# State-space constants: four 16-row products per step on four column groups of TensorE, after the step's four transposes

## The chip, the cores and the metric

One core of one Trainium2 chip runs the whole program. The metric is the device time of one execution in microseconds (us), lower is better. The kernel before has three timed runs and one profiled execution.

## The reference

The program is two transformer-like blocks on a sequence of 512 rows and 1024 columns. The change lies in the constants of the second block's state-space mixer (S5): 64 groups, each with 64 complex states and 16 inputs and outputs.

```python
def s5_mixer(u, lam_re, lam_im, log_dt, b_re, b_im, c_re, c_im, d_skip, w_glu):
    ...
    mag = jnp.exp(lr * dt)
    ab_re = mag * jnp.cos(li * dt)
    ab_im = mag * jnp.sin(li * dt)
    ...
    bb_re = coef_re[..., None] * br - coef_im[..., None] * bi
    bb_im = coef_re[..., None] * bi + coef_im[..., None] * br
    v_re = jnp.einsum('blgh,gph->blgp', uf, bb_re)
    v_im = jnp.einsum('blgh,gph->blgp', uf, bb_im)
    ...
    _, _, s_re, s_im = lax.associative_scan(_complex_affine_combine, (a_re, a_im, v_re, v_im), axis=1)
    y = (jnp.einsum('blgp,ghp->blgh', s_re, c_re.astype(jnp.float32))
         - jnp.einsum('blgp,ghp->blgh', s_im, c_im.astype(jnp.float32))
         + d_skip.astype(jnp.float32).reshape(SSM_GROUPS, SSM_GROUP) * uf)
```

The kernel runs the scan in chunks of 8 positions. For every group it needs three constant matrices that depend on the weights alone: the pole's powers times B (what a chunk's inputs add to the state), C times the pole's powers (what the state adds to a chunk's outputs), and the products C·A^l·B for l = 0 to 7, 16×16 each, with the skip weight d on the diagonal of the first (what a chunk's inputs add to its own outputs).

## The kernel before

`run` (L1616) calls `block1` and then `block2`. Work on large matrices follows one pattern: a weight tile is loaded by a DMA that SyncE (SP) issues (L98), split into a high part (ScalarE, ACT, L131) and a low part (VectorE, DVE, L132), and three matmuls (L126 to L128) make one product of nearly full precision. In the first block's feed-forward part, `up_prod` (48 matmuls for both matrices, 24 for one) alternates with bias, convolution and gate on ACT and DVE, and eight down-products of 33 matmuls follow each half.

The state-space constants are prepared in between. `s5_prep` (L987) is a generator. The feed-forward loop calls `next(prep)` at two out of every five up-products (L833, L834) and at three of the eight down-products of the first half (L852, L853), so TensorE gets one small piece of the preparation between long pieces of matmul work. There are 16 steps; a step takes GC = 4 groups:

- `front(c)` (L1007) runs on GpSimd (POOL). It makes `W`, the pole's powers times B (128×4×8×16), and `Ca`, C times the powers (128×4×9×16). Both have two buffers, so POOL works one step ahead of TensorE.
- `back(c)` (L1060) runs one call later. It writes `Ca` to `MO_d` (L1064), and per group lets TensorE do a transpose of `W` (L1071, 128×128, into `ps`) and the product of `W`'s first 16 columns with `Ca` (L1072, 16 rows × 128 columns, into `pk`, f32, no split). The four groups of a step alternate: transpose, product, transpose, product. ACT copies `ps` to `Rc` (L1074) and `pk` to `kp` (L1075); POOL writes `Rc` to `R_d` (L1076), makes the diagonal `dg` from `dT` (L1078), adds it (L1079), and writes `kp` to `K_d` (L1080).

Every second step also starts with two transposes of the next C rows (L1053). At the end eight DMAs (L1101) copy shifted pieces of `K_d` to `MO_d`. `R_d` and `MO_d` are read in `block2`, from `s5_state` and `s5_out`.

The order on each engine is set by a scheduler in the tile framework from the program's order and dependences, and instructions of one engine run in that order.

At the end of the first block the row sums of squares are made (`ss_mix`, L878) and `rstd_rows` (L311) turns them into 1/sqrt on DVE (`rsqrt_dve`, L160 to L166, `nwx`, `nwi`, `nwt`, `rstd`) and spreads them with matmuls (L322) and copies (L326, L327) to `rb_mix`, by which the first products of the second block are scaled (L1177). `block2` also has 25 small DVE instructions on 128×8 and 128×16 tiles for a lower bound (`lbm`, `lbd`, `ex`, `lbc`, `oml`, L892 to L905 and L1153 to L1161), which use no result of this neighbourhood.

Of the kernel before, what the change touches and what calls it, by code (L numbers as in the profile page):

```python
# [11 lines left out]
F32 = mybir.dt.float32  # L12
# [3 lines left out]
ALU = mybir.AluOpType  # L16
AX = mybir.AxisListType
PSUM = bass.MemoryType.PSUM

P = 128  # L20
# [49 lines left out]
class Kern:  # L70
# [837 lines left out]
    def s5_poles(self):  # L908
        nc, tc, A = self.nc, self.tc, self.A
        v = nc.vector  # L910
        self.R_d = tc.dram_tile([P, 64, P], F32, name="R_d")
        self.MO_d = tc.dram_tile([P, 64, 2 * P], F32, name="MO_d")
        NP = 18
        pt = self.s5pt = self.tmp.tile([P, NP, 64], F32, name="s5pt")
        dT = self.s5dT = self.tmp.tile([16, 64], F32, name="s5dT")
        if True:
            if True:
                dp = self.s5dpool
                t = lambda s: dp.tile([64, 64], F32, name="s5_" + s)
                lr, li, th, sn, ve = t("lr"), t("li"), t("th"), t("sn"), t("ve")  # L920
                ld, dt = dp.tile([64, 1], F32, name="s5_ld"), dp.tile([64, 1], F32, name="s5_dt")
                dd = self.s5dd = self.tmp.tile([64, 16], F32, name="s5_dd")
                nc.gpsimd.dma_start(lr, A["ssm_lambda_re_2"][0])
                nc.gpsimd.dma_start(li, A["ssm_lambda_im_2"][0])
                nc.gpsimd.dma_start(ld, A["ssm_log_dt_2"].rearrange("o g -> g o"))
                nc.gpsimd.dma_start(dd, A["ssm_d_2"][0].rearrange("(g h) -> g h", h=16))
                e2, p = self.expm1_parts(dp, ld, 64, 1)
                v.scalar_tensor_tensor(dt, p, 1.0, e2, ALU.add, ALU.mult)
                x, em = t("x"), t("em")
                v.tensor_scalar(x, lr, dt, None, ALU.mult)  # L930
                v.tensor_scalar(th, li, dt, None, ALU.mult)
                e2, p = self.expm1_parts(dp, x, 64, 64)
                v.tensor_tensor(em, p, e2, ALU.mult)
                v.scalar_tensor_tensor(em, e2, -1.0, em, ALU.add, ALU.add)
                self.sincos(dp, th, sn, ve, 64, parts=64)
                cs, nr, den, u1, u2 = t("cs"), t("nr"), t("den"), t("u1"), t("u2")
                q = dp.tile([64, NP, 1, 64], F32, name="s5_q")
                v.tensor_scalar(cs, ve, -1.0, 1.0, ALU.mult, ALU.add)
                v.tensor_tensor(nr, em, cs, ALU.mult)
                v.tensor_tensor(nr, nr, ve, ALU.subtract)  # L940
                ar, ai = q[:, 0, 0], q[:, 1, 0]
                v.tensor_scalar(ar, nr, 1.0, None, ALU.add)
                v.scalar_tensor_tensor(ai, em, 1.0, sn, ALU.add, ALU.mult)
                v.tensor_tensor(den, lr, lr, ALU.mult)
                v.tensor_tensor(u1, li, li, ALU.mult)
                v.tensor_tensor(den, den, u1, ALU.add)
                v.reciprocal(den, den)
                cr, ci = q[:, 16, 0], q[:, 17, 0]
                v.tensor_tensor(u1, nr, lr, ALU.mult)
                v.tensor_tensor(u2, ai, li, ALU.mult)  # L950
                v.tensor_tensor(u1, u1, u2, ALU.add)
                v.tensor_tensor(cr, u1, den, ALU.mult)
                v.tensor_tensor(u1, ai, lr, ALU.mult)
                v.tensor_tensor(u2, nr, li, ALU.mult)
                v.tensor_tensor(u1, u1, u2, ALU.subtract)
                v.tensor_tensor(ci, u1, den, ALU.mult)
                for l in range(2, 9):
                    a, b = l // 2, l - l // 2
                    (xr, xi), (yr, yi) = [(q[:, 2 * m - 2, 0], q[:, 2 * m - 1, 0]) for m in (a, b)]
                    zr, zi = q[:, 2 * l - 2, 0], q[:, 2 * l - 1, 0]  # L960
                    v.tensor_tensor(u1, xr, yr, ALU.mult)
                    v.tensor_tensor(u2, xi, yi, ALU.mult)
                    v.tensor_tensor(zr, u1, u2, ALU.subtract)
                    v.tensor_tensor(u1, xr, yi, ALU.mult)
                    v.tensor_tensor(u2, xi, yr, ALU.mult)
                    v.tensor_tensor(zi, u1, u2, ALU.add)
                self.s5q = q
# [19 lines left out]
    def s5_prep(self):  # L987
        nc, tc, A, pt, dT = self.nc, self.tc, self.A, self.s5pt, self.s5dT
        if True:
            sp = self.s5pool  # L990
            GC = 4
            g = nc.gpsimd
# [6 lines left out]
            g.dma_start(bw[64:], bre)  # L999
            g.tensor_scalar(bw[:64], bw[:64], -1.0, None, ALU.mult)  # L1000
            cre, cim = [A[n][0].rearrange("(c g) h p -> (g h) c p", c=8) for n in ("ssm_c_re_2", "ssm_c_im_2")]
            K_d = tc.dram_tile([16, 64, 240], F32, name="K_d")
            kp = sp.tile([16, GC, 240], F32, name="s5_kp")
            g.memset(kp, 0.0)
            cs8 = None

            def front(c):  # L1007
# [36 lines left out]
            def c_load(c2):  # L1044
                raw = craw[c2] = sp.tile([P, 3, 64], F32, tag="s5_cr", bufs=2, name=self.nm("s5cr"))
                for i, src in enumerate((cre, cim, cre)):
                    nc.sync.dma_start(raw[:, i], src[:, c2])

            def c_rows(c2):
                raw = craw.pop(c2)  # L1050
                ps = self.aux()
                for i in range(2):
                    nc.tensor.transpose(ps[:, i * P : i * P + P], raw[:, i : i + 2].rearrange("p a b -> p (a b)"), self.ident)  # L1053
                cs = nxt[c2] = sp.tile([P, 2, 8, 16], F32, tag="s5_cs8", bufs=2, name=self.nm("s5cs8"))
                p4 = ps[:, : 2 * P].rearrange("p (s g h) -> p s g h", s=2, h=16)
                nc.scalar.copy(cs[:64, 0], p4[:64, 0])
                nc.scalar.mul(cs[64:, 0], p4[64:, 0], -1.0)
                nc.scalar.mul(cs[:, 1], p4[:, 1], -1.0)

            def back(c, W, Ca):  # L1060
                g0 = c * GC
                gs = slice(g0, g0 + GC)
                tl = lambda s, shp, b=1: sp.tile(shp, F32, tag="s5_" + s, bufs=b, name=self.nm("s5" + s))
                g.dma_start(self.MO_d[:, gs, P:].rearrange("p g (l h) -> p g l h", h=16), Ca[:, :, 1:, :])  # L1064
                Rc = tl("Rc", [P, GC, P])
                for h in range(GC // 4):
                    ps = self.aux()
                    pk = self.aux()
                    for i in range(4):
                        gi = 4 * h + i  # L1070
                        nc.tensor.transpose(ps[:, i * P : i * P + P], W[:, gi].rearrange("p l h -> p (l h)"), self.ident)  # L1071
                        nc.tensor.matmul(pk[:16, i * P : i * P + P], lhsT=W[:, gi, 0, :], rhs=Ca[:, gi, :8, :].rearrange("p l h -> p (l h)"), start=True, stop=True)  # L1072
                    hs = slice(4 * h, 4 * h + 4)
                    nc.scalar.copy(Rc[:, hs], ps.rearrange("p (g x) -> p g x", g=4))  # L1074
                    nc.scalar.copy(kp[:, hs, 112:], pk[:16].rearrange("p (g x) -> p g x", g=4))  # L1075
                g.dma_start(self.R_d[:, gs], Rc)  # L1076
                dg = tl("dg", [16, GC, 16])
                g.tensor_tensor(dg, self.ident[:16, :16].unsqueeze(1).to_broadcast([16, GC, 16]), dT[:, gs].unsqueeze(2).to_broadcast([16, GC, 16]), ALU.mult)  # L1078
                g.tensor_tensor(kp[:, :, 112:128], kp[:, :, 112:128], dg, ALU.add)  # L1079
                g.dma_start(K_d[:, gs], kp)  # L1080

            prev = None
            c_load(0)
# [2 lines left out]
            for c in range(17):  # L1086
                yield
                if c == 0:
                    ps = self.aux()
                    nc.tensor.transpose(ps[:16, :64], self.s5dd, self.ident[:64, :64])  # L1090
                    nc.vector.tensor_copy(dT, ps[:16, :64])
                if c % 2 == 0 and c < 14:
                    c_load(c // 2 + 1)
                if c % 2 and c < 15:
                    c_rows(c // 2 + 1)
                if prev is not None:
                    back(c - 1, *prev)
                prev = front(c) if c < 16 else None
            yield
            for j in range(8):  # L1100
                g.dma_start(self.MO_d[16 * j : 16 * j + 16, :, :P], K_d[:, :, 16 * j : 16 * j + P])  # L1101


    def slot(self):
# [571 lines left out]
```

## Time and profile before

| what | value |
|---|---|
| median of three runs | 1825.73 us (1822.69, 1825.73, 1832.12) |
| profiled execution, its own time | 1825.45 us |
| its span, first to last instruction | 1823.6 us |
| TensorE matmul (PE) busy | 1738.0 us, 95% |
| VectorE / ScalarE / GpSimd busy | 59% / 43% / 18% |
| mean granted TensorE clock | 0.986 of full speed |

The profiled execution is 2 us longer than its span, and lies within 0.3 us of the median. PE is a matmul and PEld a weight load on TensorE; the two overlap, and a matmul's duration holds its latency, so what a stream of matmuls costs is read from start to start. "issue" as a releaser means that the engine waited for nothing that the profile shows.

### The profile page before, as it was taken

The numbers are of one execution on the slowest core, as the hardware profiler recorded it, in microseconds if no ns is written. First come the engines' busy times: TensorE is split into PE (matmuls) and PEld (weight loads), VectorE is DVE, ScalarE is ACT, GpSimd is POOL, SyncE is SP. The second block draws the span as 40 slices with busy tenths as digits, with TensorE's granted clock in tenths as the row PEclk, the third lists the DMA queues.
The fourth block names the chain that finished last, engine by engine and source line by source line (L and its number), as shares of the span: only waits on it lengthen the run. The fifth ranks groups of instructions, "written<-read, shape, count | busy, mean of one in ns | idle before, by whom it ended". The sixth has DMA issues, their size and how long they took to land.

```text
span 1823.6 us, 28508 instructions
## 1 busy us (share of the span) xinstructions
PE 1738.0 (95%) x11509; PEld 1525.5 (84%) x11509; DVE 1074.7 (59%) x2343; ACT 780.4 (43%) x1298; POOL 321.4 (18%) x441
## 2 busy tenths in 40 slices
PE   1989998999999999999999999999999999999998
PEld 1777755877777778899899899899999999889986
DVE  6687878986443566454488634343444466536652
ACT  2674485344332444324546834343322443324332
POOL 5000000278836841031000000200000000000001
PEclk9899998999999999999899999999999999999999
DMA  7323625353244325367432135936443222332231
GB/s 280 98 88 111 215 71 186 116 105 124 85 117 150 108 92 182 117 195 123 129 99 82 65 116 162 227 118 232 156 137 104 82 93 70 113 107 93 70 104 47
DMA packets 178766, 226.64 MB, mean 124 GB/s; under 512 B 10699, under 2 KB 146746, under 8 KB 175178
## 3 DMA queue, kind: packets, MB, share of 16 engines
q1 hardware_dynamic: 164256, 181.95, 31.5%
q0 software_dynamic: 10640, 38.19, 7.8%
q10 hardware_dynamic: 3738, 4.69, 0.7%
q8 instruction: 90, 1.47, 0.4%
q14 instruction: 42, 0.34, 0.1%
HBM read 196.29 MB, written 32.70 MB: 126 GB/s over the span
## 4 chain that ended last, share of the span: by engine, by line
PE 69%; issue 12%; DVE 9%; ACT 4%; DMA 4%; POOL 1%; ACTq 0%; SPq 0%; POOLq 0%; DVEq 0%
PE pp L126 18%; PE pp L127 17%; PE pp L128 17%; DVE wl L132 2%; DMA wraw<-in_w_in_dram 2%; PE pd L128 1%; PE pd L126 1%; PE pd L127 1%; PE aux L1072 1%; PE aux L1354 1%; PE aux L442 1%; PE aux L126 1%; PE aux L128 1%; PE aux L127 1%; PE pv L455 1%
## 5 line engine op out<-in xcount | busy, mean ns | idle before, releaser
L126 PE MATMUL pp<-s,wh 128*128 128x258 f32 (+2 forms) x1856 | 543.2, 293 | 8.6 <-ACT sg L1427 4.5
L127 PE MATMUL pp<-s,wh 128*128 128x258 f32 (+2 forms) x1856 | 527.9, 284 | 0.0
L128 PE MATMUL pp<-s,wl 128*128 128x258 f32 (+2 forms) x1856 | 525.5, 283 | 0.0
L132 DVE TENSOR_TENSOR wl<-wraw,wh 128x1024 fp32r<-128x1024 f32 (+4 forms) x260 | 302.9, 1178 | 190.4 <-ACT wh L131 189.4
L131 ACT CAST wh<-wraw 128x1024 fp32r<-128x1024 f32 (+4 forms) x260 | 245.0, 964 | 338.0 <-PE pp L127 203.4
L126 PEld LDWEIGHTS pp<-s,wh 128*128 128x128 f32 x1856 | 352.2, 190 | 13.3 <-ACT sg L1427 4.7
L127 PEld LDWEIGHTS pp<-s,wh 128*128 128x128 f32 x1856 | 352.9, 190 | 0.2 <-DVE s L333 0.2
L128 PEld LDWEIGHTS pp<-s,wl 128*128 128x128 f32 x1856 | 352.4, 190 | 0.1
L126 PE MATMUL pp<-h2H,wh 128*128 128x512 f32 x336 | 133.5, 397 | 2.4 <-DVE cy L846 2.4
L127 PE MATMUL pp<-h2L,wh 128*128 128x512 f32 x336 | 133.2, 396 | 1.1 <-DVE h2L L343 1.1
L128 PE MATMUL pp<-h2H,wl 128*128 128x512 f32 x336 | 132.1, 393 | 0.0
L126 PEld LDWEIGHTS pp<-h2H,wh 128*128 128x128 f32 x336 | 63.1, 188 | 20.1 <-ACT aH L131 2.8
L127 PEld LDWEIGHTS pp<-h2L,wh 128*128 128x128 f32 x336 | 63.0, 188 | 16.1 <-DVE h2L L343 2.2
L128 PEld LDWEIGHTS pp<-h2H,wl 128*128 128x128 f32 x336 | 63.2, 188 | 14.2
L126 PE MATMUL pp<-aH,wh 128*128 128x512 f32 x176 | 70.1, 398 | 0.0
L127 PE MATMUL pp<-aL,wh 128*128 128x512 f32 x176 | 69.8, 396 | 0.0
L128 PE MATMUL pp<-aH,wl 128*128 128x512 f32 x176 | 69.8, 396 | 0.0
L1592 POOL TENSOR_TENSOR ht<-ht,gf 128x512 f32<-128x512 f32 x4 | 5.7, 1438 | 344.7 <-ACT fsq L1590 344.7
L126 PE MATMUL pp<-wh,hH 128*128 128x512 f32 (+1 forms) x160 | 62.3, 389 | 1.2 <-ACT hH L525 1.2
L1556 DVE TENSOR_TENSOR xz<-pp,rb_f 128x516 f32<-128x516 f32 x44 | 30.6, 696 | 54.2 <-PE pp L128 54.2
L127 PE MATMUL pp<-wl,hH 128*128 128x512 f32 (+1 forms) x160 | 61.9, 387 | 0.5 <-DVE wl L132 0.5
L128 PE MATMUL pp<-wh,hL 128*128 128x512 f32 (+1 forms) x160 | 61.4, 384 | 0.0
(592 smaller groups left out, 3462.0 us busy)
## 6 DMA issues: line engine op xcount, KB each, us to landing
wraw<-in_w_up_dram SPq DMA_DIRECT2D x40, 1024.0 KB, 5.2
wada<-in_w_ada_dram SPq DMA_DIRECT2D x24, 1024.0 KB, 4.9
wraw<-in_w_in_dram SPq DMA_DIRECT2D x17, 1024.0 KB, 12.3
wraw<-in_w_down_dram SPq DMA_DIRECT2D x16, 704.0 KB, 4.6
wraw<-in_w_in_dram SPq DMA_DIRECT2D x22, 512.0 KB, 5.4
wraw<-in_w_down_dram SPq DMA_DIRECT2D x8, 1024.0 KB
wraw<-MO_d SPq DMA_DIRECT2D x6, 896.0 KB
xraw<-in_w_in_dram SPq DMA_DIRECT2D x10, 512.0 KB, 7.7
```

The costliest lines, as they stand in the source:

```text
L126: mm(ps, lhsT=sh, rhs=mh, start=start, stop=False)
L127: mm(ps, lhsT=sh, rhs=ml, start=False, stop=False)
L128: mm(ps, lhsT=sl, rhs=mh, start=False, stop=stop)
L131: self.nc.scalar.copy(H, x)
L132: self.nc.vector.tensor_tensor(L, x, H.bitcast(F32), ALU.subtract)
L442: nc.tensor.transpose(ps[:, w : w + P], probs[i][:, j * P : (j + 1) * P], self.ident)
L455: self.nc.tensor.matmul(pv[64 * a : 64 * a + 64, j * P :], lhsT=vs[a](j), rhs=ptrs[a][j], start=(j == 0), stop=(j == NT - 1), skip_group_c ...
L1072: nc.tensor.matmul(pk[:16, i * P : i * P + P], lhsT=W[:, gi, 0, :], rhs=Ca[:, gi, :8, :].rearrange("p l h -> p (l h)"), start=True, stop=True)
L1354: nc.tensor.matmul(p3[:n, c, 32 * i : 32 * i + 32], lhsT=lhs, rhs=ch(Q1)[:, c, 32 * i : 32 * i + 32], start=True, stop=True)
L1556: nc.vector.tensor_tensor(xz, ps, rb, ALU.mult)
L1592: nc.gpsimd.tensor_tensor(h, h, gf[:, :512], ALU.mult)
```

## The change

A step's four transposes now come first, and its four products after them. Each product takes 32 columns of `W` (two powers, of which the second is not used) and writes to its own 32 partitions of one PSUM tile, so that each uses its own quarter of TensorE's columns. `kp`, `dg`, `dT` and `K_d` are laid out accordingly: group i of a step on partitions 32i to 32i+15, the other 16 rows unused. The copy of the products is 128×128 and no longer 16×512; the write to `K_d` has 128 rows of 240 and no longer 16 rows of 960. A constant `eye` (four 32×32 unit matrices, one above the other) is made once by a DVE reduction.

```diff
-        dT = self.s5dT = self.tmp.tile([16, 64], F32, name="s5dT")
+        dT = self.s5dT = self.tmp.tile([P, 16], F32, name="s5dT")
...
-                dd = self.s5dd = self.tmp.tile([64, 16], F32, name="s5_dd")
+                dd = self.s5dd = self.tmp.tile([16, 4, 32], F32, name="s5_dd")
+                nc.gpsimd.memset(dd, 0.0)
...
-            K_d = tc.dram_tile([16, 64, 240], F32, name="K_d")
-            kp = sp.tile([16, GC, 240], F32, name="s5_kp")
+            K_d = tc.dram_tile([16, P, 240], F32, name="K_d")
+            kp = sp.tile([P, 240], F32, name="s5_kp")
             g.memset(kp, 0.0)
+            eye = sp.tile([P, 32], F32, name="s5_eye")
+            nc.vector.tensor_reduce(eye, self.ident.rearrange("p (i r) -> p r i", r=32), AX.X, ALU.add)
...
-                for h in range(GC // 4):
-                    ps = self.aux()
-                    pk = self.aux()
-                    for i in range(4):
-                        gi = 4 * h + i
-                        nc.tensor.transpose(ps[:, i * P : i * P + P], W[:, gi].rearrange("p l h -> p (l h)"), self.ident)
-                        nc.tensor.matmul(pk[:16, i * P : i * P + P], lhsT=W[:, gi, 0, :], rhs=Ca[:, gi, :8, :].rearrange("p l h -> p (l h)"), start=True, stop=True)
-                    hs = slice(4 * h, 4 * h + 4)
-                    nc.scalar.copy(Rc[:, hs], ps.rearrange("p (g x) -> p g x", g=4))
-                    nc.scalar.copy(kp[:, hs, 112:], pk[:16].rearrange("p (g x) -> p g x", g=4))
+                ps = self.aux()
+                pk = self.aux()
+                for i in range(GC):
+                    nc.tensor.transpose(ps[:, i * P : i * P + P], W[:, i].rearrange("p l h -> p (l h)"), self.ident)
+                for i in range(GC):
+                    nc.tensor.matmul(pk[32 * i : 32 * i + 32, :P], lhsT=W[:, i, :2].rearrange("p l h -> p (l h)"), rhs=Ca[:, i, :8, :].rearrange("p l h -> p (l h)"), start=True, stop=True, skip_group_check=True)
+                nc.scalar.copy(Rc, ps.rearrange("p (g x) -> p g x", g=4))
+                nc.scalar.copy(kp[:, 112:], pk[:, :P])
                 g.dma_start(self.R_d[:, gs], Rc)
-                dg = tl("dg", [16, GC, 16])
-                g.tensor_tensor(dg, self.ident[:16, :16].unsqueeze(1).to_broadcast([16, GC, 16]), dT[:, gs].unsqueeze(2).to_broadcast([16, GC, 16]), ALU.mult)
-                g.tensor_tensor(kp[:, :, 112:128], kp[:, :, 112:128], dg, ALU.add)
-                g.dma_start(K_d[:, gs], kp)
+                dg = tl("dg", [P, 16])
+                g.tensor_scalar(dg, eye[:, :16], dT[:, c : c + 1], None, ALU.mult)
+                g.tensor_tensor(kp[:, 112:128], kp[:, 112:128], dg, ALU.add)
+                g.dma_start(K_d[c], kp)
```

On TensorE the step changes like this. Before, at the first step (`aux_4280` holds the transposes, `aux_4281` the products):

```order
L1053 MATMUL aux_4271<-ident,s5cr_4159 128x128 x2
L1071 MATMUL aux_4280<-ident,s5W_4164 128x128
L1072 MATMUL aux_4281<-s5Ca_4165,s5W_4164 16x128
L1071 MATMUL aux_4280<-ident,s5W_4164 128x128
L1072 MATMUL aux_4281<-s5Ca_4165,s5W_4164 16x128
L1071 MATMUL aux_4280<-ident,s5W_4164 128x128
L1072 MATMUL aux_4281<-s5Ca_4165,s5W_4164 16x128
L1071 MATMUL aux_4280<-ident,s5W_4164 128x128
L1072 MATMUL aux_4281<-s5Ca_4165,s5W_4164 16x128
L126 MATMUL pp_4314<-h2H,wh_4150 128x512
```

And now, at the same place (L1057, L1073 and L1075 are the new numbers of L1053, L1071 and L1072):

```order
L128 MATMUL pp_4245<-h2H,wl_4146 128x512
L1057 MATMUL aux_4274<-ident,s5cr_4162 128x128 x2
L1073 MATMUL aux_4283<-ident,s5W_4167 128x128 x4
L1075 MATMUL aux_4284<-s5Ca_4168,s5W_4167 32x128 x4
L126 MATMUL pp_4317<-h2H,wh_4153 128x512
```

The neighbours of the step are the same matmuls as before, in all 16 steps; within it four alternations have become one.

The scheduler has also moved work that the diff does not name. On DVE, at the change from the first block to the second, this stood before (from the sums of squares to the copy that spreads the result; the last `rstd` row comes after two more rounds like the one shown):

```order
L878 COPY ss_mix<-aux_6962 128x5
L1389 MEMSET ss_1400_8097 128x5
L160 TENSOR_SCALAR nwx_7041<-ss_mix 128x5
L161 TENSOR_SCALAR nwi_7043<-nwx_7041 128x5
L164 TENSOR_TENSOR nwt_7042<-nwi_7043 128x5
L165 SCALAR_TENSOR_TENSOR nwt_7042<-nwt_7042,nwx_7041 128x5
```

And now (L1155 to L1157 are the new numbers of L1153 to L1155):

```order
L878 COPY ss_mix<-aux_6965 128x5
L1155 TENSOR_TENSOR lbm<-vcols_157 128x8
L160 TENSOR_SCALAR nwx_7044<-ss_mix 128x5
L1156 TENSOR_TENSOR lbd<-vcols_157,lbm 128x8
L1157 TENSOR_TENSOR lbd<-vcols_157,lbm 128x8
L161 TENSOR_SCALAR nwi_7046<-nwx_7044 128x5
L892 TENSOR_SCALAR ex_7009<-lbd 128x16
L164 TENSOR_TENSOR nwt_7045<-nwi_7046 128x5
L893 TENSOR_SCALAR ex_7009<-ex_7009 128x16
L165 SCALAR_TENSOR_TENSOR nwt_7045<-nwt_7045,nwx_7044 128x5
```

The lower-bound instructions stood some 85 instructions earlier, among the up-products; they now stand in and behind the chain that ends in `rstd`: 15 between `ss_mix` and the last `rstd`, and some ten behind it, ahead of the copies to `rb_mix`. The new reduction for `eye` stands in the like chain of the first block (between L160 and L161 there). Two matmuls that stood behind the spreading matmuls L322 at the change of blocks now stand ahead of them.

## Rows read from the trace of the kernel before

**Rows 1.** The page, part 1: busy time, share, instructions of TensorE's matmuls

```profile
PE 1738.0 (95%) x11509; PEld 1525.5 (84%) x11509; DVE 1074.7 (59%) x2343; ACT 780.4 (43%) x1298; POOL 321.4 (18%) x441
```

**Rows 2.** Stretches: start:end, length, busy PE, PEld, DVE, ACT, POOL; PEclk, DMA share

```profile
411.00:680.00 269.00, 269.00 (x1195) 202.04 (x1194) 141.08 (x153) 104.39 (x164) 176.49 (x259) 1.00 0.37 113
680.00:780.00 100.00, 100.00 (x431) 80.59 (x429) 55.47 (x102) 38.70 (x64) 7.48 (x11) 1.00 0.49 149
```

**Rows 3.** The chain that ended last, its longest pieces: two neighbours in the list

```profile
404.83 0.67 DVE cy L846
780.39 0.76 DVE x L859
```

**Rows 4.** Waits of TensorE's weight loads, 405 to 690 us: total, times, longest

```profile
PEld aux L1071 <- issue: 10.2, 48, 0.2
PEld aux L1072 <- issue: 3.6, 15, 0.3
...
PEld pp L126 <- DVE wl L132: 0.6, 3, 0.2
```

**Rows 5.** Timeline of TensorE's matmuls, first step: start, length, instruction, count

```profile
411.50 0.27 PE L1071 MATMUL aux<-ident,s5W 128*128 128x128 f32 x1
411.70 0.39 PE L1072 MATMUL aux<-s5Ca,s5W 128*16 128x128 f32 x2
412.02 0.33 PE L1071 MATMUL aux<-ident,s5W 128*128 128x128 f32 x1
...
413.44 0.39 PE L1072 MATMUL aux<-s5Ca,s5W 128*16 128x128 f32 x2
413.76 0.50 PE L126 MATMUL pp<-h2H,wh 128*128 128x512 f32 x1
```

**Rows 6.** Groups by line and shape: the products, matmuls and weight loads

```profile
L1072 PE MATMUL aux<-s5Ca,s5W 128*16 128x128 f32 x128 | 25.1, 278 | 0.0
...
L1072 PEld LDWEIGHTS aux<-s5Ca,s5W 128*16 128x16 f32 x128 | 7.1, 94 | 9.6 <-issue 3.6 <-POOL s5t L1035 0.2
```

**Rows 7.** Timeline of TensorE: 32 transposes of this size in a row

```profile
1441.89 3.66 PE L1535 MATMUL aux<-ident,hT 128*128 128x128 f32 x32
```

**Rows 8.** Products on two column groups: one burst, its first 0.03 us, the line's durations

```profile
879.61 0.97 PE L1205 MATMUL aux<-U,xraw 128*64 128x66 f32 x24
...
879.61 0.28 PE L1205 MATMUL aux<-U,xraw 128*64 128x66 f32 x2
...
L1205 PE MATMUL aux<-U,xraw x96: 222/222/273, 879.6 to 895.6; 128*64 128x66 f32 x96
```

**Rows 9.** Timeline of POOL and TensorE, the eleventh step

```profile
580.63 2.15 POOL L1036 TENSOR_TENSOR s5Ca<-s5Ca,s5t 128x512 f32<-128x512 f32 x1
...
592.68 0.27 PE L1071 MATMUL aux<-ident,s5W 128*128 128x128 f32 x1
```

**Rows 10.** Groups by line and shape: POOL's writes of a step to DRAM

```profile
L1076 POOL DMA_DIRECT2D R_d<-s5Rc x16 | 9.3, 581 | 17.4 <-ACT s5Rc L1074 17.4
L1080 POOL DMA_DIRECT2D K_d<-s_kp x16 | 8.5, 531 | 0.6 <-POOL s_kp L1079 0.6
```

**Rows 11.** Groups by line and shape: a DVE reduction of 128 elements per partition

```profile
L874 DVE TENSOR_REDUCE sqm<-sqm 128x16 f32<-128x128 f32 x1 | 0.4, 366 | 0.0
```

**Rows 12.** Timeline of DVE (and TensorE, third row): change of blocks; then lower-bound instructions

```profile
784.44 0.17 DVE L878 COPY ss_mix<-aux 128x5 f32<-128x5 f32 x1 [1.15 <-PE aux L308]
786.66 0.17 DVE L166 SCALAR_TENSOR_TENSOR rstd<-nwt,rstd 128x5 f32<-128x5 f32 x1
786.97 1.45 PE L322 MATMUL aux<-ident,rstd 16*128 16x16 f32 x10 [0.26 <-DVE rstd L166]
...
790.05 1.18 DVE L1177 TENSOR_TENSOR us<-pp,rb_mix 128x528 f32<-128x528 f32 x1 [0.92 <-PE pp L128]
...
682.52 0.17 DVE L1154 TENSOR_TENSOR lbd<-vcols,lbm 128x8 f32<-128x8 f32 x1
682.61 0.16 DVE L1155 TENSOR_TENSOR lbd<-vcols,lbm 128x8 f32<-128x8 f32 x1
```

More of the change, by code (lines that the diff above doesn't have):

```diff
@@ L925, in s5_poles @@
                 nc.gpsimd.dma_start(ld, A["ssm_log_dt_2"].rearrange("o g -> g o"))
-                nc.gpsimd.dma_start(dd, A["ssm_d_2"][0].rearrange("(g h) -> g h", h=16))
+                nc.gpsimd.dma_start(dd[:, :, :16], A["ssm_d_2"][0].rearrange("(c i h) -> c i h", i=4, h=16))
                 e2, p = self.expm1_parts(dp, ld, 64, 1)
@@ L1089, in s5_prep @@
                     ps = self.aux()
-                    nc.tensor.transpose(ps[:16, :64], self.s5dd, self.ident[:64, :64])
-                    nc.vector.tensor_copy(dT, ps[:16, :64])
+                    nc.tensor.transpose(ps[:, :16], self.s5dd.rearrange("c i r -> c (i r)"), self.ident[:16, :16])
+                    nc.vector.tensor_copy(dT, ps[:, :16])
                 if c % 2 == 0 and c < 14:
@@ L1100, in s5_prep @@
             for j in range(8):
-                g.dma_start(self.MO_d[16 * j : 16 * j + 16, :, :P], K_d[:, :, 16 * j : 16 * j + P])
+                g.dma_start(self.MO_d[16 * j : 16 * j + 16, :, :P], K_d.rearrange("c (i r) x -> r (c i) x", r=32)[:16, :, 16 * j : 16 * j + P])
     def slot(self):
```

## The prediction

> **What bounds the kernel now.** I first read the busy times on the page: TensorE's matmuls are busy for 95% of the span and no other engine for more than 59% [rows 1]. So work taken from TensorE can count, if it lies where TensorE never waits. Second, the stretches: in the 269 us that hold the 16 steps TensorE is busy for all 269.00, and for all 100.00 of the next 100, at the full granted clock (2.4 GHz), while DVE, ACT and POOL have from a third to two thirds of the time [rows 2]. Third, the chain that ended last: among its longest pieces nothing stands between a DVE piece at 404.83 and one at 780.39 [rows 3]; in between it runs along TensorE in short pieces. What a step gets shorter there moves everything behind it forward. Fourth, the waits of the weight loads, where the reader is to see that the steps are expensive beyond their matmuls: 48 transposes, three per step, begin 0.2 us late, 10.2 us in all, with nothing that releases them [rows 4].
>
> The timeline of one step shows where that comes from [rows 5]. The first transpose starts at 411.50, the first product at 411.70, the next transpose at 412.02. A product is two records (f32 takes two passes); together they take 0.39 us against 278 ns for one [rows 6], so the second pass starts 0.11 after the first. From its start to the next transpose or main matmul there are 0.32 − 0.11 = 0.21 us: TensorE empties before it goes back from a 16-column product to the full width. A pair costs 0.58 us (from 412.02 on, three pairs end at 413.76), the step from its first transpose to the next main matmul 413.76 − 411.50 = 2.26 us. All 16 steps are alike, so 36 us of the span go to them.
>
> **The change part by part.**
>
> *The transposes.* Four in a row, with no product between. 32 of this shape in a row take 3.66 us with the last one's latency of 0.27, that is (3.66 − 0.27)/31 = 0.109 us each [rows 7]. The fourth starts 0.33 us after the first, and the first product 0.20 behind it, as in the first pair [rows 5]: 0.53.
>
> *The products.* Eight passes (four products, two each), 0.11 us apart if they share columns. They no longer do: each product has a quarter of the columns. The trace of before has no four column groups, but two: L1205 has 12 products on two halves, 24 passes of 66 columns. The burst takes 0.97 us, of which the last pass's latency is 0.222, so passes start (0.97 − 0.222)/23 = 0.033 us apart, where 0.11 × 66/128 = 0.057 would be the pace on shared columns. And two passes stand in its first 0.03 us, started within some 0.01 us [rows 8], although the program puts both products of one half ahead of the first of the other. So each group of columns takes its own passes as soon as it can. Carried to four groups: four first passes 0.01 apart, each second pass 0.11 behind its first, the last start 0.03 + 0.11 = 0.14 us after the first product's. The other bound is no overlap: 7 × 0.11 = 0.78. I take 0.14, since the burst on two groups is the nearest row and shows full overlap, and keep 0.78 for the range.
>
> *The way back.* One return to full width per step and no longer four: 0.21.
>
> The new step is 0.53 + 0.14 + 0.21 = 0.88 us against 2.26, a gain of 1.38 us, and 16 × 1.38 = 22.1 us. Without overlap it is 0.53 + 0.78 + 0.21 = 1.52, a gain of 0.74, 11.8 us in all. Most of the gain is not the columns but three emptyings less per step.
>
> The Trainium skill ("TensorE: Matmul & The Clock Gate", Part 3) says that matmuls on different tiles start about 4 ns apart, but also that they start and end strictly in program order. By the second rule a product's first pass could not overtake the second pass of the one before, the last start would be 3 × 0.11 + 0.11 = 0.45 and the gain 16 × 1.07 = 17.1 us. The burst's first two starts [rows 8] speak against it; it is kept as a rival.
>
> *ACT and POOL.* ACT's copy of the products becomes 128×128. ACT is busy 104 of 269 us [rows 2]: nothing. POOL's write to K_d has 128 rows instead of 16 and may go from 531 ns to some 581, as R_d's 128 rows have [rows 10]: 16 × 0.05 = 0.8 us on POOL. POOL is a step ahead: the eleventh step's last operand is ready at 580.63 + 2.15 = 582.78, and TensorE takes it at 592.68 [rows 9], 9.9 us later, the smallest such lead I found among the steps. Even all 22 us of the gain, spread over 16 steps, take 1.4 us from each, and POOL gets its buffers back as much earlier. Nothing. If that cover went, the next transposes would wait for W.
>
> *The reduction for eye* stands in the chain on DVE that the first block's feed-forward part waits for. A reduction of the same number of elements took 366 ns [rows 11]. Between dependent small instructions some of it is covered: 0.2 us lost, bounds 0 and 0.4.
>
> *The lower-bound instructions* move into the chain from the sums of squares to rstd. That chain goes from 784.44 to 786.66 + 0.17 = 786.83, and TensorE is waiting for it (0.26 us idle before L322) [rows 12]. Behind the wait stand the scaled products of the second block. An independent small instruction follows its neighbour by 0.09 us (682.52 to 682.61 [rows 12]), inside the 0.2 that dependent ones need, so one between two links costs nearly nothing and two cost some 0.1; there are four such pairs: 0.4 us. If all 15 cost their full 0.2, it is 3.0. The ten behind the chain delay the copies to rb_mix by up to 2 us, of which TensorE's 1.45 us of spreading [rows 12] cover most. I take 0.4 for all, bounds 0 and 3. The two matmuls moved ahead of L322 only fill the idle time.
>
> **The sum.** 22.1 − 0.2 − 0.4 = 21.5 us. Against the profiled execution, 1825.45 us, which is within 0.3 of the median of 1825.73, that gives 1804.0 us, 1.2% less.
>
> **The rivals.**
>
> *Staggered products*, in program order (above): 17.1 − 0.6 = 16.5, 1809 us. For it: a product's two passes are neighbours in the program. Against it: rows 8.
>
> *The change does not do what it says*: the column groups do not run side by side, only the emptyings go. 11.8 − 0.6 = 11.2, 1814 us. For it: no row shows quarter widths. Against it: rows 8 again.
>
> *The gain is given back downstream.* TensorE asks for the split weights earlier; DVE's low parts came late three times already, 0.6 us in all [rows 4]. DVE is busy 141 of 269 us and ACT 104 [rows 2], so only some arrivals could be late. If more than about half is returned, the time is between 1815 and 1825. Little speaks for it.
>
> *The loads do not overlap.* If a pass needs its weight load finished alone, 0.094 us [rows 6] come to each pass's 0.11: 0.53 + 7 × 0.21 + 0.21 = 2.21, a gain of 0.05 per step, no change: 1825 us. The Trainium skill says this in the same Part 3 of that page: a weight load overlaps a running matmul only if the row groups differ, and here all products use all 128 rows. The burst's 0.033 us per pass, loads included and on all rows too, contradicts it.
>
> *Every pass empties the array* before the next quarter of columns may start, at the price of the return seen above, 0.11 + 0.21 = 0.32 per pass: 0.53 + 7 × 0.32 + 0.21 = 2.98 us per step, 0.72 more than now, 11.5 us over 16 steps: 1837 us. It decides on the spacing of the passes: above (2.26 − 0.53 − 0.21)/7 = 0.217 us the step is longer than before. For it: going between widths does cost an emptying. Against it: halves alternate without one [rows 8].
>
> **How the numbers follow.** Chances: overlap as forecast 0.45, staggered 0.20, not side by side 0.15, given back 0.12, loads apart 0.04, every pass empties 0.04. The range of 1800 to 1817 us takes in the first three, with 4 us below the forecast for the scatter of single runs (from 1822.69 to 1832.12 before) and 3 above the third. A measurement here can tell about 0.5%, 9 us, from no change. Faster by more: the first two, most of the third (its 11.2 is close to the bound) and a little of the fourth, 0.78. Slower by more: the last, 0.04. The same: the rest, 0.18.
>
> **What would show it.** In the profile after, a step from first transpose to the next main matmul near 0.9 us (1.2 if staggered, 1.5 if one after the other); the issue waits of the transposes gone from the weight loads; TensorE busy without a gap from 411 to the end of the block, which should come some 22 us earlier than 780; the idle time before L322 within 0.5 us of the 0.26 now. Steps above 2 us, or steps of 0.9 with the lost time found in waits for wl or W further on, would make the prediction wrong.

## The result, and the profile after

The changed kernel takes 1805.07 us (median of four runs, 1802.17 to 1809.47), the kernel before beside it 1826.6 (four runs, 1822.69 to 1832.12): a ratio of 0.9881 with a 95% interval of 0.9859 to 0.9902, 1.2% less, 21.5 us between the medians. The forecast was 1804.0 us, 1.2% less. The profiled execution took 1805.34 us with a span of 1803.5 us.

The rows after answer to those of before in the order of the groups. First the page's busy times, answering to [rows 1], and the stretch of the 16 steps, answering to [rows 2]:

```profile
PE 1718.0 (95%) x11509; PEld 1521.1 (84%) x11509; DVE 1074.6 (60%) x2344; ACT 776.2 (43%) x1298; POOL 328.5 (18%) x442
```

```profile
411.00:680.00 269.00, 269.00 (x1285) 214.14 (x1285) 156.48 (x170) 107.17 (x177) 193.99 (x274) 0.99 0.41 133
411.00:764.00 353.00, 353.00 (x1646) 281.73 (x1645) 201.37 (x237) 140.46 (x232) 193.99 (x274) 1.00 0.42 132
```

The number of matmuls is the same, 11509, and TensorE is busy 20 us less. In the 269 us in which it ran 1195 matmuls before it now runs 1285, without a gap, and there is none up to 764 us. The same two pieces of the chain as in [rows 3]:

```profile
409.91 0.67 DVE cy L846
764.40 0.76 DVE x L859
```

Between them lie 354.49 us; before they were 780.39 − 404.83 = 375.56 us. The stretch has become 21.07 us shorter, and that is the place where the time went. It begins 5.08 us later (5.3 us are there already at `nwx`, where the first block's chain to `rstd` begins, before the steps) and what lies behind it is 4.11 us shorter (1803.5 − 764.40 = 1039.10 against 1823.6 − 780.39 = 1043.21). Further profiles below show that the later start is scatter, and that 1.3 us of the shorter rest are not.

The step, where [rows 5] had 2.26 us (timeline of TensorE's matmuls, first step; L1073 and L1075 are the transposes and the products):

```profile
418.16 0.60 PE L1073 MATMUL aux<-ident,s5W 128*128 128x128 f32 x4
418.69 0.43 PE L1075 MATMUL aux<-s5Ca,s5W 128*32 128x128 f32 x8
419.04 0.50 PE L126 MATMUL pp<-h2H,wh 128*128 128x512 f32 x1
419.38 0.39 PE L127 MATMUL pp<-h2L,wh 128*128 128x512 f32 x1
```

From the first transpose to the first product it is 0.53 us, from there to the main matmul 0.35, together 0.88; all 16 steps are 0.88 or 0.89. What had started by 418.75 us (timeline of a narrow stretch):

```profile
418.69 0.32 PE L1075 MATMUL aux<-s5Ca,s5W 128*32 128x128 f32 x4
```

Of the eight passes four had started, and the burst of these four is 0.32 us long, that of all eight 0.43. The first passes last 0.30 us and the last ones 0.27 (0.285 in the mean, below), so the fourth started 0.02 us after the first and the last one 0.15 us after it, 0.20 ahead of the main matmul. The narrow stretches show no start between 418.72 and 418.81. The products' matmuls and weight loads, answering to [rows 6] (groups by line and shape):

```profile
L1075 PE MATMUL aux<-s5Ca,s5W 128*32 128x128 f32 x128 | 6.8, 285 | 0.0
...
L1075 PEld LDWEIGHTS aux<-s5Ca,s5W 128*32 128x32 f32 x128 | 2.5, 108 | 2.7 <-issue 2.5 <-POOL s5Ca L1040 0.2
```

A matmul still lasts 285 ns (278 before), but all of them together cover 6.8 us of TensorE's time and no longer 25.1.

Waits of the weight loads from 405 to 690 us, answering to [rows 4]:

```profile
PEld aux L1075 <- issue: 2.5, 15, 0.2
PEld pp L126 <- issue: 2.4, 12, 0.2
PEld pp L126 <- ACT wh L131: 0.6, 3, 0.2
PEld pp L126 <- DVE cy L849: 0.2, 1, 0.2
PEld aux L1075 <- POOL s5Ca L1040: 0.2, 1, 0.2
```

The transposes' 48 waits of 10.2 us are gone; one wait per step is left at the products (15 + 1) and one at the main matmul behind them (12 + 3 + 1). All are 0.2 us long, whichever engine they are put down to. Last, the change of blocks, answering to [rows 12] (timeline of DVE, and TensorE in the last row, with its idle time and what ended it):

```profile
768.44 0.17 DVE L878 COPY ss_mix<-aux 128x5 f32<-128x5 f32 x1 [1.15 <-PE aux L308]
768.52 0.16 DVE L1155 TENSOR_TENSOR lbm<-vcols 128x8 f32<-128x8 f32 x1
768.64 0.17 DVE L160 TENSOR_SCALAR nwx<-ss_mix 128x5 f32<-128x5 f32 x1
...
771.18 1.45 PE L322 MATMUL aux<-ident,rstd 16*128 16x16 f32 x10 [0.25 <-DVE ex L902]
```

From `ss_mix` to L322 it is 2.74 us, before 2.53. TensorE starts 19 matmuls in this time, before 17, and the first `us` of the second block (L1177, now L1179) starts 5.56 us behind `ss_mix`, before 790.05 − 784.44 = 5.61 [rows 12].

### The profile page after: what moved, and what is told of

It is laid out like the page before. It is cut to its first block, busy times and chain, and to the rows that moved or that the text cites. A ratio compares the mean times of both kernels' runs of the same rounds, so it can differ in the third digit from the quotient of the medians.

```text
span 1803.5 us, 28508 instructions
## 1 busy us (share of the span) xinstructions
PE 1718.0 (95%) x11509; PEld 1521.1 (84%) x11509; DVE 1074.6 (60%) x2344; ACT 776.2 (43%) x1298; POOL 328.5 (18%) x442
## 4 chain that ended last, share of the span: by engine, by line
PE 72%; issue 12%; DVE 6%; ACT 5%; DMA 4%; POOL 1%; ACTq 0%; POOLq 0%; DVEq 0%
PE pp L126 19%; PE pp L127 18%; PE pp L128 18%; DMA y_d<-s 1%; PE pd L126 1%; PE pd L128 1%; PE pd L127 1%; PE aux L1356 1%; PE aux L127 1%; PE aux L128 1%; PE aux L126 1%; DVE wl L132 1%; ACT s L1232 1%; PE pp L412 1%; PE aux L442 1%
```

## The experiments

Each kernel was timed beside the kernel before on the same chip, in five rounds ("products first" in three). The kernel before differs by a few us from one chip to the next, so ratios are compared. What a change does on TensorE is read from all 16 visits of a profile: a visit lasts from the start of the last main matmul ahead of a step to the start of the second main matmul behind it, so that it holds both changes of width and the transposes of C's rows.

| kernel | median us (before beside it) | ratio, 95% | 16 steps, us | 16 visits, us |
|---|---|---|---|---|
| before | | | 36.26 | 46.94 |
| the change | 1805.07 (1826.6) | 0.9881 (0.9859 to 0.9902) | 14.16 | 24.82 |
| order alone | 1811.0 (1822.64) | 0.9935 (0.9922 to 0.9948) | 24.10 | 34.81 |
| column groups alone | 1824.66 (1822.64) | 1.0018 (1.0002 to 1.0033) | 37.17 | 47.84 |
| two column groups | 1806.26 (1822.64) | 0.9908 (0.9894 to 0.9923) | 17.52 | 28.22 |
| the change again | 1799.86 (1822.64) | 0.9883 (0.9863 to 0.9903) | 14.16 | 24.81 |
| full width | 1809.57 (1824.78) | 0.9908 (0.9888 to 0.9928) | 19.96 | 30.31 |
| pairs of steps | 1803.66 (1824.78) | 0.9882 (0.9859 to 0.9905) | 11.70 | 22.17 |
| products first | 1801.62 (1824.78) | 0.9873 (0.9845 to 0.9902) | 12.31 | 24.04 |
| pairs, products first | 1804.22 (1829.23) | 0.9874 (0.9853 to 0.9896) | 10.71 | 21.80 |
| the change, third time | 1803.67 (1829.23) | 0.9860 (0.9837 to 0.9884) | 14.15 | 24.81 |

**The order alone.**

```diff
                         nc.tensor.transpose(ps[:, i * P : i * P + P], W[:, gi].rearrange("p l h -> p (l h)"), self.ident)
+                    for i in range(4):
+                        gi = 4 * h + i
                         nc.tensor.matmul(pk[:16, i * P : i * P + P], lhsT=W[:, gi, 0, :], ...
```

> The kernel before with the order alone changed: per step the four transposes first, then the four 16-column products, all four on the same columns of TensorE. Theory of the prediction (three emptyings less per step, passes on shared columns 0.11 us apart): a step from its first transpose to the next main matmul takes 0.53 + 7 x 0.11 + 0.21 = 1.51 us, 16 x (2.26 - 1.51) = 12 us less than before, about 1814 us. Rival A (the order does all of it, four column groups add nothing): 0.9 us per step and some 1804 us, as after. Rival B (each product empties the array behind it, whatever follows): a step of 0.53 + 4 x 0.32 = 1.8 us, 7 us less than before, about 1819.

The first step of its profile:

```profile
416.13 0.60 PE L1071 MATMUL aux<-ident,s5W 128*128 128x128 f32 x4
416.66 1.05 PE L1074 MATMUL aux<-s5Ca,s5W 128*16 128x128 f32 x8
417.64 0.50 PE L126 MATMUL pp<-h2H,wh 128*128 128x512 f32 x1
```

The step is 1.51 us, the 16 are 12.2 us shorter than before, and the ratio makes 0.65% or 12 us. The first rival falls: the order gives a little over half, and the columns the rest. The second falls too: four products in a row empty TensorE once.

**The column groups alone.** The second loop of the changed kernel is dropped, so that each product follows its transpose.

```diff
-                for i in range(GC):
-                    nc.tensor.matmul(pk[32 * i : 32 * i + 32, :P], ...
+                    nc.tensor.matmul(pk[32 * i : 32 * i + 32, :P], ...
```

> The changed kernel with the column groups alone: 32-column products on four column groups, but each again between two transposes. Theory of the prediction: the column groups can't overlap when a transpose at full width stands between, so a pair stays at 0.58 us and the step at 2.26 us; the time is that of before, 1825 to 1828 us. Rival (passes of different column groups overlap whatever stands between, so the columns do it): a step of about 1.5 us or less, 1814 us or less.

```profile
415.18 0.27 PE L1073 MATMUL aux<-ident,s5W 128*128 128x128 f32 x1
415.38 0.41 PE L1074 MATMUL aux<-s5Ca,s5W 128*32 128x128 f32 x2
415.71 0.33 PE L1073 MATMUL aux<-ident,s5W 128*128 128x128 f32 x1
...
417.50 0.50 PE L126 MATMUL pp<-h2H,wh 128*128 128x512 f32 x1
```

No gain: with a transpose between them the column groups never run side by side. The step is even 0.06 us longer than before (2.32), 0.9 us in all, and the median 0.18% higher, with an interval that reaches down to 0.02%, so that the 0.9 us of the steps lie in it. (This kernel also has the 1.3 us that the changed kernel gains in the second block, told below; steps and gain together would make it 0.4 us shorter than before, just outside the interval, and what makes it longer is not known.) So the 9.9 us that the columns add behind the new order need the order first.

**Two column groups.** Products 0 and 2 on one, 1 and 3 on the other, in the order A, A, B, B.

```diff
-                for i in range(GC):
-                    nc.tensor.matmul(pk[32 * i : 32 * i + 32, :P], ...
+                for i in (0, 2, 1, 3):
+                    a, f = 32 * (i % 2), P * (i // 2)
+                    nc.tensor.matmul(pk[a : a + 32, f : f + P], ...
...
-                nc.scalar.copy(kp[:, 112:], pk[:, :P])
+                nc.scalar.copy(kp[:64, 112:], pk[:64, :P])
+                nc.scalar.copy(kp[64:, 112:], pk[:64, P : 2 * P])
```

> The changed kernel with its products on two column groups and no longer four, in the order A, A, B, B; ACT copies the result in two pieces. Theory of the prediction (each column group takes its own passes as soon as it can, whatever the order): four passes per group 0.11 apart, both groups at once: 0.53 + 3 x 0.11 + 0.01 + 0.21 = 1.08 us per step, 16 x (2.26 - 1.08) = 18.9 us less than before, about 1807 us. Rival A (passes start in the order of the program): B's first pass follows A's last start, 0.53 + 0.33 + 0.01 + 0.33 + 0.21 = 1.41 us per step, about 1812. Rival B (nothing overlaps): 1.51, about 1814.

A step, and then what had started by 603.92 and by 604.01 us:

```profile
603.32 0.60 PE L1073 MATMUL aux<-ident,s5W 128*128 128x128 f32 x4
603.85 0.64 PE L1076 MATMUL aux<-s5Ca,s5W 128*32 128x128 f32 x8
604.41 0.50 PE L126 MATMUL pp<-h2H,wh 128*128 128x512 f32 x1
```

```profile
603.85 0.31 PE L1076 MATMUL aux<-s5Ca,s5W 128*32 128x128 f32 x2
603.85 0.42 PE L1076 MATMUL aux<-s5Ca,s5W 128*32 128x128 f32 x4
```

1.09 us, as the free column groups give it (1.08), and not 1.41. Two passes start within 0.02 us of each other, two more some 0.13 us later, and the last of the eight 0.64 − 0.27 = 0.37 us after the first, although two products of one group, four passes, stand ahead of the other group's first in the program; the scheduler left the products in this order. The trace does not name a pass's column group, but passes on shared columns start 0.11 us apart (the order alone, above), so of the two at the start one must be B's, and it starts ahead of A's second, third and fourth. That the instructions of one engine run in the order that the scheduler sets, as the section on the kernel before has it, does not hold for passes on different column groups. The time, 0.92% or 16.8 us less, goes with the 18.7 us of the steps within its interval. The Trainium skill ("TensorE: Matmul & The Clock Gate", Part 3) has matmuls start strictly in program order; these rows differ from it, and they decide.

**The full width.** As the order alone, with products that use all 128 columns of W as weights, so that the width never changes.

```diff
-                        nc.tensor.matmul(pk[:16, i * P : i * P + P], lhsT=W[:, gi, 0, :], ...
+                        nc.tensor.matmul(pk[:, i * P : i * P + P], lhsT=W[:, gi].rearrange("p l h -> p (l h)"), ...
```

> The kernel before with the four transposes first and then four products at the full width of TensorE: each takes all 128 columns of W as weights, of whose 128 result rows the first 16 are used. This prices the change of width by itself. Theory (the 0.21 us and the 0.09 us ahead of the first product belong to a change of width): twelve passes at 0.109 us with nothing between them, 1.31 us per step, and the main matmul behind it takes its usual 0.23 us to the next and no longer 0.34; 16 x (2.60 - 1.54) = 17 us less than before, though twice as many TensorE columns are used as in the order-alone run and none side by side. Rival (the price belongs to the products themselves or to the turn to another PSUM tile, whatever the width): 1.51 us per step and 0.34 behind it, as with the order alone, 12 us less than before.

```profile
414.89 0.60 PE L1071 MATMUL aux<-ident,s5W 128*128 128x128 f32 x4
415.33 1.06 PE L1074 MATMUL aux<-s5Ca,s5W 128*128 128x128 f32 x8
416.14 0.48 PE L126 MATMUL pp<-h2H,wh 128*128 128x512 f32 x1
416.45 0.39 PE L127 MATMUL pp<-h2L,wh 128*128 128x512 f32 x1
```

The split came out otherwise than written (1.25 us to the main matmul and 0.31 behind it, not 1.31 and 0.23: that matmul starts only 0.03 us behind the last pass), but the sum is 1.56 against 1.54 expected, and 16.6 us less than before over the visits; the time says 0.92%, 16.8 us. The same eight passes on 16 columns, with the order alone, take (34.81 − 30.31)/16 = 0.28 us more per visit. That is the price of going to a narrow width and back, 0.09 ahead of the first product and 0.2 behind the last, and it belongs to the width. The kernel before, which goes there and back four times per step, agrees: (46.94 − 30.31)/16 = 1.04 us, 0.26 each time. Eight times the columns (not twice, as I had written) and none side by side, and it still beats the narrow products on shared columns.

**Pairs of steps, and products first.** Three versions that might beat both kernels. For pairs, the first step's 32 columns of W are copied and a third buffer of Ca is kept, and in every second step eight products stand together; the second moves the products ahead of the transposes; the third does both. With pairs `K_d` is also written once per two steps, and 16 DMAs and no longer eight copy it at the end.

```diff
+                if c % 2:
+                    for j, (w, ca) in enumerate((held[0], (W, Ca))):
+                        for i in range(GC):
+                            nc.tensor.matmul(pk[32 * i : 32 * i + 32, j * P : j * P + P], lhsT=w[:, i, :2]...
+                else:
+                    Wk = tl("Wk", [P, GC, 2, 16])
+                    nc.scalar.copy(Wk, W[:, :, :2])
+                    held[0] = (Wk, Ca)
```

> A version that may beat both kernels: on the changed kernel, the products of two steps stand together in every second step, eight products on four column groups; the other steps have transposes alone. A copy of the first step's 32 columns of W and a third buffer of Ca hold its operands over. Theory (a change of width is paid once per visit): a step without products 4 x 0.109 = 0.44 us and 0.23 to the second main matmul behind it, a step with eight products 0.53 + 0.03 + 3 x 0.11 + 0.21 = 1.10 and 0.34 behind it; a pair 2.11 us, where two steps of the changed kernel take 2 x 1.22 = 2.44: 8 x 0.33 = 2.6 us less than the changed kernel, which only the steps can show, 24 to 25 us less than before. Rival (later operands or copies make TensorE wait): new waits of the weight loads at the steps, and no gain on the changed kernel.

> The changed kernel with the four products ahead of the four transposes. Theory (two changes of width per step, whatever stands on either side): the sum from the first product to the second main matmul behind the step stays at 1.22 us within 0.05, and the time is that of the changed kernel. Rival (the return is cheaper where transposes follow, since the 0.34 us that the first main matmul then takes to the next becomes the usual 0.23): 1.16 us or less, 1 us less in all.

> Both small steps at once on the changed kernel: the products of two steps in one visit, and ahead of that step's transposes. By the steps of the two runs before: 2.6 us less than the changed kernel from the pairs, and 0.05 us less for each of the 8 visits from the order, 0.4 us; 3.0 us in all, 24 us less than the kernel before. Rival: ACT's copy of W or the later operands make TensorE wait at a step, and the steps give less than 2 us. The median may not tell 3 us from nothing; the steps must.

A visit with eight products ahead of the transposes, from the last kernel's profile:

```profile
427.04 0.42 PE L1075 MATMUL aux<-s5Ca,s5Wk 128*32 128x128 f32 x8
427.28 0.40 PE L1075 MATMUL aux<-s5Ca,s5W 128*32 128x128 f32 x8
427.61 0.66 PE L1077 MATMUL aux<-ident,s5W 128*128 128x128 f32 x4
428.02 0.48 PE L126 MATMUL pp<-h2H,wh 128*128 128x512 f32 x1
```

The visits are 2.65 us shorter with pairs than in the changed kernel (expected 2.6), 0.8 shorter with the products first, 3.0 with both (expected 3.0). "Products first" was not expected rightly: I had the sum from the first product at 1.22 us, and it is 1.08, since the 0.09 us of going narrow now lies ahead of that product; counted over the whole visit the gain is 0.05 us, near the rival's 0.06. No new wait appears at a step. The medians can't tell these versions from the changed kernel: 1804.22 us with both against 1803.67 on the same chip, intervals that overlap. The profiles show where the 3 us of the pairs may have gone: ahead of the first step TensorE waits 3.2 us for `cy` L846 in both, and 2.35 us in the changed kernel, and both have a wait of 1.1 us in the second block that the changed kernel has not (below). Whether the pairs cause either is not shown.

**The changed kernel twice more.**

> The changed kernel once more, for the time beside the other runs on the same chip and a second profile of it. By the first profile: a step of 0.88 to 0.89 us, 22.1 us less in the 16 steps than before, 20 to 22 us less in all. If the first half's later start (5 us at the first up-product) and the earlier end (4 us between the first block's end and the last instruction) are scatter, they come out otherwise here, while the steps stay within 0.02 us.

> The changed kernel a third time, to set the version with pairs beside it on one chip: 20 to 22 us less than before, steps of 0.88 to 0.89 us and 14.16 us in all 16.

The steps are the same to 0.01 us in sum. From the piece `cy` L846 to `x` L859 of the chain it took 354.49, 352.92 and 354.45 us, while the start of that stretch lay at 409.91, 407.08 and 414.02, and the rest behind it took 1039.10, 1036.80 and 1037.43 us. Over all eleven profiles the start lies between 404.83 and 414.02 and the rest between 1036.8 and 1043.2, with the kernel before at one end of both. "Products first", which has the changed kernel's work ahead of the steps, starts at 404.99, so the later start is scatter. The rest is longer in none of the three than before, so nothing was given back behind the steps.

But 1.3 us of the shorter rest are no scatter. From `ss_mix` to the first product of L1205 it is 95.18 us before and 93.84 to 93.85 in all three profiles of the changed kernel, since one wait of TensorE in the second block is gone there. Before, it looks like this:

```profile
820.41 0.36 PE L126 MATMUL pp<-zuH,wh 128*128 128x264 f32 x1 [1.09 <-DVE us L1177]
```

"Column groups alone" and "products first" lack this wait too (93.84 to 93.86 us); order alone, full width and both versions with pairs have it (95.13 to 95.16). In these ten profiles the wait is missing exactly where the scheduler moved the lower-bound instructions on DVE. "Two column groups" breaks the rule: they are moved, and TensorE waits twice (96.06 us). So the wait goes with the scheduler's new order on DVE and not with the steps; which instruction decides it is not shown. What then remains of the 4.11 us may be TensorE's clock: in the profile of the kernel before it was at the lower level for some 20 us behind `x` and ahead of the program's last 10 us, in those of the changed kernel for 7 to 10.

## Why the prediction was right, point by point

**The step.** Forecast 0.53 + 0.14 + 0.21 = 0.88 us; measured 0.53 + 0.15 + 0.20 in the first step, and 0.88 or 0.89 in all 16. That the parts meet to 0.01 us is partly luck: the second pass of a product in [rows 5] starts 0.12 us after the first and not 0.11, since the first pass lasts 0.28 us and the second 0.27, and the same 0.01 was then too much in the way back. Two sums in the prediction are 0.01 too high (7 × 0.11 is 0.77, 3 × 0.11 + 0.11 is 0.44) and move nothing. The gain of the steps, forecast 22.1, is 36.26 − 14.16 = 22.10 us. Each part was tried by itself: without the columns 1.51 us (1.52 forecast), with two groups 1.09, without the change of width no emptying.

**That most of the gain is emptyings** held, narrowly: 12.2 of 22.1 us come with the order alone, 9.9 with the columns. The prediction's two bounds, 0.74 and 1.38 us per step, are the order alone (0.76) and the whole change (1.38).

**Carrying the two-group burst [rows 8] to four groups**, the choice on which the forecast stood, was right: four passes start within 0.02 us. The rivals with staggered products, with no overlap, with weight loads that don't overlap and with an emptying per pass all fall by that row and by the two-group run. For the loads, all eight of a step start within 0.05 us of each other while passes run, on the same 128 rows; the Trainium skill's rule (the same part of that page) that they overlap only on different row groups is not borne out here.

**The gain given back** did not happen, and the row that spoke for it was misread. The three late low parts of DVE [rows 4] were no late operands: with 11 waits put down to "issue" and two to `cy` they make 16 waits of 0.2 us ahead of the main matmul, one per step, which is the price of the return to full width. In the changed kernel three of the 16 are put down to ACT's `wh` instead, at the same length.

**ACT and POOL at nothing.** The copy of the products became faster (278 ns, 570 before), the write to `K_d` slower, 572 ns where 581 was expected [rows 10], and TensorE waits for neither: the only POOL wait at a step is 0.2 us, once, as long as the 15 others at the products.

```profile
L1082 POOL DMA_DIRECT2D K_d<-s_kp x16 | 9.1, 572 | 0.6 <-POOL s_kp L1081 0.6
L1077 ACT COPY s_kp<-aux 128x128 f32<-128x128 f32 x16 | 4.4, 278 | 2.5 <-DMA K_d<-s_kp 2.5
```

**The eye reduction, forecast 0.2 us, cost nothing.** The first block's chain on DVE, and TensorE's spreading of its result, first before and then with the reduction:

```profile
371.04 0.16 DVE L160 TENSOR_SCALAR nwx<-aux 128x4 f32<-128x4 f32 x1 [1.70 <-PE aux L308]
373.77 1.16 PE L322 MATMUL aux<-ident,rstd 128*128 128x128 f32 x8
...
376.33 0.16 DVE L160 TENSOR_SCALAR nwx<-aux 128x4 f32<-128x4 f32 x1 [2.12 <-PE aux L308]
376.41 0.36 DVE L1008 TENSOR_REDUCE s_eye<-ident 128x32 f32<-128x128 f32 x1
376.69 0.15 DVE L161 TENSOR_SCALAR nwi<-nwx 128x4 int32<-128x4 int32 x1
379.06 1.16 PE L322 MATMUL aux<-ident,rstd 128*128 128x128 f32 x8
```

`nwx` to `nwi` is 0.36 us, where it was 0.19, so the chain on DVE is 0.17 longer. But TensorE starts L322 2.73 us behind `nwx` in both: it is busy with other matmuls until then, and the last `rstd` is ready 0.61 us ahead before and still 0.45 ahead now. The prediction had the feed-forward part wait for this chain; TensorE does not wait for it here.

**The lower-bound instructions, forecast 0.4 us, cost TensorE nothing either.** The chain to `rstd` did become 2.74 − 2.53 = 0.21 longer. Where the scheduler left them ahead of the up-products the chain is 2.52 us (order alone) and 2.53 (full width and both versions with pairs), where it moved them 2.73 to 2.74 (the change three times, column groups alone, two column groups, products first). But TensorE fills these 0.21 us with the two matmuls that moved ahead of L322, 0.12 us each: its idle time before L322 stayed at 0.25, and the first `us` comes 0.05 us earlier than before. The prediction saw these two matmuls and did not count that they are then done.

**The sum** was to be 21.5. With the measured terms it is 22.10 from the steps, nothing for the two others, and 1.3 from the wait in the second block, which was not foreseen: 23.4 us. The medians give 21.5 (0.9881 of 1826.6 is 21.7 less, with an interval from 17.9 to 25.8; the two repeats give 1.2% and 1.4%, 21.3 and 25.6 us). So the mechanism and the size of the steps are shown by the profiles, but that forecast and medians agree to a tenth of a us is luck. The profiled stretch from `cy` to `x` holds none of the other terms, and is to be set beside 22.1; that it shows 21.07 is TensorE's clock, below.

## What to carry to other kernels

A narrow matmul between wide ones costs more by changing the width (0.26 to 0.28 us here) than by its passes (two of 0.11): collect the narrow ones behind the wide ones first, and only then put them on column groups of their own, since groups overlap only where nothing wide stands between them. Where they can't be collected, products at full width that throw columns away may be cheaper (the run at full width had them collected, so this is not shown). Once the changes of width are few, count what is left before going on: here two more ways to save them gave 3 us of 1804 that only the steps of a trace could show. And look at the places that the edit does not name: an order that the scheduler moved on another engine was worth 1.3 us here, and a longer chain off TensorE's path nothing.

## What was not expected of the hardware

A pass on a free column group overtakes passes that stand ahead of it in the program, as the two-group run shows.

Going narrow costs something too, 0.09 us, and the two ways together 0.28 us; the prediction had the first part inside its 0.20 without naming it.

TensorE's clock made part of the scatter. Just ahead of the first step TensorE waits for `cy` L846, and at the end of that wait the granted clock fell to the lower level, 1.2 GHz, for some 3 us. Stretches of the changed kernel's first profile (columns as in [rows 2]), and its timeline of TensorE there:

```profile
408.00:411.00 3.00, 0.65 (x3) 0.31 (x2) 3.00 (x5) 1.83 (x3) 2.84 (x6) 0.99 0.66 196
411.00:414.00 3.00, 3.00 (x8) 2.32 (x8) 3.00 (x5) 1.54 (x3) 2.92 (x4) 0.50 0.45 154
```

```profile
410.72 0.59 PE L126 MATMUL pp<-h2H,wh 128*128 128x512 f32 x1 [2.35 <-DVE cy L846]
411.11 0.63 PE L127 MATMUL pp<-h2L,wh 128*128 128x512 f32 x1
411.54 0.63 PE L128 MATMUL pp<-h2H,wl 128*128 128x512 f32 x1
...
414.44 0.40 PE L126 MATMUL pp<-h2H,wh 128*128 128x512 f32 x1
414.68 0.40 PE L127 MATMUL pp<-h2L,wh 128*128 128x512 f32 x1
```

Matmuls that take 0.23 us from start to start took 0.43 there. This wait stands in all eleven profiles, 2.3 to 2.4 us long in eight, 3.2 in both versions with pairs and 4.5 with the order alone; the clock fell at it in nine, and not in that of the kernel before nor in one of the changed kernel. If one takes the 16 visits from the stretch from `cy` to `x`, the two without a fall have 328.6 and 328.1 us left, the six with a fall of some 3 us 329.6 to 330.0, and the three with the longer waits, where it lasted some 7 us, 330.7 to 331.1. So a profile may be 1 to 3 us longer or shorter for this alone; why the clock fell in six of the eight with the short wait and not in the two others stays open.
